# Moving the first sum of weights of 21 seven-product groups from VectorE to GpSimd

## The chip, the cores and the metric

The kernel runs as one program on one core of a Trainium2 chip. The metric is the device time of one execution in microseconds (us). The core has a matrix engine (TensorE, PE in the profile; its weight loads are listed as PEld), a vector engine (VectorE, DVE), a scalar engine (ScalarE, ACT), a general engine (GpSimd, POOL) and an engine that here does nothing but issue transfers (SyncE, SP). Each engine works through its own list of instructions in the order in which the program issued them, and waits on semaphores for the others.

## The reference

One layer of a diffusion backbone is computed for 128 context tokens and 128 latent tokens of width 2048: modulation, one wide input projection, two attention mixers, a merge, an output projection, and a feed-forward part with hidden width 8192. All of it is float32. What the change touches is the first half of the feed-forward part:

```python
def sq_relu_mlp(h, w_up, w_down):
    return jnp.square(jax.nn.relu(h @ w_up)) @ w_down

h2 = rms_norm(xp, norm2_w[l]) * (1 + sc2) + sh2
xp = xp + g2 * sq_relu_mlp(h2, w_up[l], w_down[l])
```

`h2` has 128 rows for each of the two token sets, `w_up` is 2048 x 8192 and `w_down` is 8192 x 2048.

## The kernel before

**Steps.** Weights are streamed. One step is one tile of 128 x 1024 float32 (512 KB): SP loads it into a buffer called `raw`, other engines prepare it, TensorE uses it. `add_step` puts a step on the list `wsteps` and `run` walks the list. For step i, `run` first issues the loads that are due (the digit string RUN says how many steps ahead), then the preparation of all steps up to i + LOOK[i] + 1 (LOOK is a digit string too, mostly 3 to 6 in the part that matters here), then the matmuls of step i, then whatever was hung on that step. This order of issue is the order on every engine; no scheduler changes it (`manual_schedule`).

**Precision.** A weight tile is split in two: ScalarE copies it to the type float32r (`wH`, the high part), and VectorE subtracts this from the tile (`wL`, the low part, line 230). Activations are split in the same way. Every product is then three matmuls: high by high, high by low, low by high. In 13 steps listed in LO_DMA the low part is made in another way: ScalarE writes minus the high part (line 236), and a transfer issued by GpSimd adds the weight to it in memory (`minus_plus`, line 237).

**Feed-forward.** The hidden width is taken in 8 pieces of 1024 columns, each as two blocks of 512. Piece p goes through an up stage, in which `h2 @ w_up` is made, and a down stage, in which it is multiplied into four column blocks of the output (`down_unit`). In the up stages of pieces 1 to 7 the eight positions of the inner dimension are of two kinds. At a plain position two weight tiles are used as they are (24 matmuls in two steps). At the positions listed in FAST a 2 x 2 block product is made with seven products in place of eight (21 matmuls in two steps). Such a group takes two tiles `X` and `Y`, and sums of weights have to be made first. There are 36 groups: 4, 5, 5, 5, 6, 5 and 6 in pieces 1 to 7.

**A group's preparation.** `prep_x` issues one ScalarE copy (`XH`). `prep_y` issues, in this order: on ScalarE half a copy of Y (`YB`, line 1045 by way of the helper at line 83); on VectorE the first sum `t13` = X + Y's left half repeated (line 1046, 128 x 1024); on ScalarE its high part `tH`; on VectorE three operations of 128 x 512 (lines 1049 to 1051), the first of which reads `t13`; on ScalarE the high part `uH`; on VectorE the three low parts `XL`, `tL`, `uL` (lines 1054 to 1056, 128 x 1024 each). `mm_x` and `mm_y` then use them: `XL` is read by the first matmuls of the group's x step, `tL` and `uL` in its y step. The tile `t13` is called `t` in the profile, X and Y are both called `raw`.

**GpSimd's list.** During the feed-forward part GpSimd has only transfers to issue: in 16 of the down units (SUM_DMA) a transfer that adds the unit's result to the running sum (line 1137), after ScalarE has copied that result out of the accumulators, and the transfers of line 237. All tiles of 128 x 1024, loaded, split and summed ones, come from one pool of 48 buffers of 4 KB per partition (`G`), so that an instruction that writes a tile also waits for whatever last used its buffer.

Of the kernel before, what the change touches and what calls it, by code (L numbers as in the profile page):

```python
# [34 lines left out]
FAST = {1: (0, 3, 5, 7), 2: (0, 2, 3, 6, 7), 3: (0, 2, 4, 5, 7), 4: (0, 2, 4, 5, 7), 5: (0, 1, 2, 3, 5, 7), 6: (0, 3, 4, 5, 7), 7: (0, 1, 2, 4, 6, 7)}  # L35
# [8 lines left out]
RUN = "210002222232246656665644343333334454433433345555544455434445554445665555555665443433234334444445665543321222222222444444444444442222222232333344444455544544444444443344343334455533344444444443255444444455556866544443566553333323333345552332222222223444332333333333332211122222332233322211233323323333333333333333332343322211333343333333333333444433543333322233333333322333233322222222322333443434455544333120222222222222344566655555455445322325335553333333"  # L44
CONST_AT = [59, 67]
XL_DMA = []
ADA_AT = [None, 4, 12, 21, 21, 32, 32, 37]
XS_AT = {1: 9, 2: 14, 3: 30}
POST = {('kvA', 0): [67, 68, 74], ('qA', 0): [70, 73, 75], ('qA', 1): [74, 76, 82], ('kB', 0): [76, 81, 87], ('qB', 0): [83, 84, 92], ('kB', 1): [84, 89, 92], ('qB', 1): [91, 94, 97]}
# [12 lines left out]
def tile_hybrid_step(ctx: ExitStack, tc: tile.TileContext, a):  # L62
# [8 lines left out]
    act, dve, pe, pool, sync = nc.scalar, nc.vector, nc.tensor, nc.gpsimd, nc.sync  # L71

    def G(name, dt=F32):
        return gp.tile([P, 1024], dt, name=name, tag="g")
# [7 lines left out]
    def copy(out, in_):  # L82
        act.activation(out, in_, AF.Copy)  # L83
# [311 lines left out]
    def mod_pair(f):  # L395

        box, k0 = {}, 2 * f
        if f == 0:
# [10 lines left out]
            return  # L409
        i = ADA_AT[f]  # L410
        for j in range(2):
# [569 lines left out]
    def up_pair(p):  # L981
# [32 lines left out]
        for pos, is_fast in enumerate(kinds):  # L1014
# [16 lines left out]
            def prep_x(b=b, pos=pos):  # L1031
                b["XH"] = G("XH", F32R)
                copy(b["XH"], b["x"]["raw"])
                if 8 * p + pos in XL_DMA:
                    b["XL"] = G("XL", F32R)
                    minus_plus(b["XL"], b["XH"], b["x"]["src"])

            def prep_y(b=b, pos=pos):
                X, Y = b["x"].pop("raw"), b["y"].pop("raw")
                b["YB"] = G("YB", F32R)  # L1040
                if "XL" not in b:
                    b["XL"] = G("XL", F32R)
                b["tH"], b["tL"], b["uH"], b["uL"] = (G(n, F32R) for n in ("tH", "tL", "uH", "uL"))
                t = G("t13")
                copy(b["YB"][:, 0:512], Y[:, 512:1024])
                dve.tensor_tensor(t.rearrange("p (a n) -> p a n", a=2), X.rearrange("p (a n) -> p a n", a=2),  # L1046
                                  Y[:, 0:512].unsqueeze(1).to_broadcast([P, 2, 512]), op=OP.add)
                copy(b["tH"], t)
                dve.tensor_tensor(Y[:, 0:512], t[:, 0:512], X[:, 512:1024], op=OP.add)
                dve.tensor_tensor(b["YB"][:, 512:1024], Y[:, 512:1024], b["YB"][:, 0:512].bitcast(F32), op=OP.subtract)  # L1050
                dve.tensor_tensor(Y[:, 512:1024], Y[:, 0:512], Y[:, 512:1024], op=OP.add)  # L1051
                copy(b["uH"], Y)
                if 8 * p + pos not in XL_DMA:
                    dve.tensor_tensor(b["XL"], X, b["XH"].bitcast(F32), op=OP.subtract)  # L1054
                dve.tensor_tensor(b["tL"], t, b["tH"].bitcast(F32), op=OP.subtract)
                dve.tensor_tensor(b["uL"], Y, b["uH"].bitcast(F32), op=OP.subtract)
# [45 lines left out]
            for i, (nm, pf, mf) in enumerate((("x", prep_x, mm_x), ("y", prep_y, mm_y))):  # L1102
                add_step(a["w_upF"][p - 1, j, i], mf, key)
                b[nm] = wsteps[-1]
                wsteps[-1]["prep"] = pf
# [253 lines left out]
```

## Time and profile before

| what | value |
|---|---|
| median of 3 runs | 1353.36 us (1353.11 to 1353.66) |
| the profiled execution, its own time | 1353.49 us |
| its span, first to last instruction | 1351.7 us |
| up stages of pieces 1 to 7, us from the start of the span | 703-745, 790-831, 876-916, 962-1002, 1046-1087, 1132-1172, 1218-1258 |
| VectorE's first sum (line 1046) | 36 times 1218 ns |
| ScalarE's high part of that sum (`tH`, line 83) | 36 times 1063 ns |
| GpSimd's compute instructions after 662 us | none |

The first group of a piece is prepared during the down stage ahead of it (piece 1's at 693.7 us). All durations come from one profiled execution, so sums are made against its own 1353.49 us. Times in the profile are microseconds from the first instruction. A matmul's listed duration (0.39 us) overlaps the next one's; the rate of TensorE is read from the distance of their starts. VectorE's neighbours overlap slightly in the same way: instructions listed with 1.22 us start 1.13 to 1.14 us apart when nothing holds them up. A note in brackets behind an instruction gives the idle time of its engine ahead of it, and what ended that.

### The profile page before, as it was taken

How to read it: one execution, taken by the hardware profiler on the slowest of the kernel's cores; microseconds unless marked ns; L12 is line 12 of the kernel's file. 1: busy time of each engine (PE TensorE's matmuls, PEld its weight loads, DVE VectorE, ACT ScalarE, POOL GpSimd, SP SyncE). 2: the span in 40 equal slices, each digit the busy share in tenths (PEclk: the TensorE clock that was granted, in tenths of full speed). 3: DMA queues.
4: the chain of work that ended last, by engine and by line, in shares of the span. 5: the costliest groups of instructions: out<-in, count | busy, mean ns of one | idle time of the engine just before them, and what ended most of it. 6: DMA issues, size and time to landing. Idle time of an engine off the chain costs nothing. (4 is left out here: it accounts for less than half of the span.)

```text
span 1351.7 us, 18516 instructions
## 1 busy us (share of the span) xinstructions
PE 1339.3 (99%) x6699; PEld 1086.3 (80%) x6701; DVE 1156.1 (86%) x1499; ACT 730.8 (54%) x955; POOL 60.0 (4%) x71
## 2 busy tenths in 40 slices
PE   8999999999999999999999999999999999999998
PEld 4777786888888878888888888888888888888887
DVE  4578787988798979997779998998999999899685
ACT  4534532476646535345657566566665656656640
POOL 0000000422000000000000000000000000000000
PEclk9999999999999999999999999999999999999999
DMA  9999979948568999998556666988786887769942
GB/s 379 408 409 408 401 278 321 353 147 306 179 263 318 345 407 372 354 328 277 202 203 218 249 224 229 294 272 289 234 285 218 264 286 210 279 190 312 343 151 94
DMA packets 108027, 381.78 MB, mean 282 GB/s; under 512 B 12192, under 2 KB 13152, under 8 KB 107936
## 3 DMA queue, kind: packets, MB, share of 16 engines
q1 hardware_dynamic: 103200, 364.00, 73.4%
q0 software_dynamic: 4592, 16.52, 6.4%
q8 instruction: 52, 0.85, 0.3%
q14 instruction: 39, 0.32, 0.1%
q10 hardware_dynamic: 144, 0.08, 0.0%
HBM read 365.06 MB, written 7.11 MB: 275 GB/s over the span
## 5 line engine op out<-in xcount | busy, mean ns | idle before, releaser
L230 DVE TENSOR_TENSOR wL<-raw,wH 128x1024 fp32r<-128x1024 f32 x370 | 440.4, 1221 | 106.9 <-ACT wH L83 98.3
L83 ACT ACTIVATE wH<-raw 128x1024 fp32r<-128x1024 f32 x384 | 387.3, 1053 | 165.4 <-PE acc L281 31.0
L375 PE MATMUL acc<-wH,hH 128*128 128x512 f32 x288 | 113.6, 394 | 0.6 <-ACT hH L83 0.6
L377 PE MATMUL acc<-wH,hL 128*128 128x512 f32 x288 | 112.3, 390 | 0.0
L376 PE MATMUL acc<-wL,hH 128*128 128x512 f32 x288 | 112.2, 389 | 0.0
L280 PE MATMUL acc<-wH,hH 128*128 128x512 f32 x256 | 101.3, 396 | 0.0
L282 PE MATMUL acc<-wH,hL 128*128 128x512 f32 x256 | 99.8, 390 | 0.0
L281 PE MATMUL acc<-wL,hH 128*128 128x512 f32 x256 | 99.7, 389 | 0.0
L83 ACT ACTIVATE tH<-t 128x1024 fp32r<-128x1024 f32 x36 | 38.3, 1063 | 67.5 <-DVE t L1046 62.7
L375 PEld LDWEIGHTS acc<-wH,hH 128*128 128x128 f32 x288 | 54.0, 188 | 15.1 <-issue 3.3
L377 PEld LDWEIGHTS acc<-wH,hL 128*128 128x128 f32 x288 | 54.1, 188 | 11.9 <-DVE hL L87 0.4
L376 PEld LDWEIGHTS acc<-wL,hH 128*128 128x128 f32 x288 | 54.1, 188 | 10.8
L1200 DVE CUSTOM_DVE_ANT_0 aT<-aT,cB,cols 128x1024 f32<-128x1024 f32 x48 | 61.1, 1281 | 0.2
L1200 DVE CUSTOM_DVE_ANT_0 junk<-aT,cB,cols 128x1024 bf16<-128x1024 f32 x48 | 61.2, 1284 | 0.0
L83 ACT ACTIVATE uH<-raw 128x1024 fp32r<-128x1024 f32 x36 | 38.3, 1063 | 35.3 <-DVE raw L1051 32.4
L282 PEld LDWEIGHTS acc<-wH,hL 128*128 128x128 f32 x256 | 48.0, 188 | 10.1
L281 PEld LDWEIGHTS acc<-wL,hH 128*128 128x128 f32 x256 | 48.1, 188 | 9.4
L280 PEld LDWEIGHTS acc<-wH,hH 128*128 128x128 f32 x256 | 48.1, 188 | 9.5
L297 PE MATMUL ps_ada<-araw,cpad 128*32 128x256 f32 x768 | 46.4, 382 | 3.6 <-DMA araw<-in_w_pair 3.0
L1046 DVE TENSOR_TENSOR t<-raw 128x1024 f32<-128x1024 f32 x36 | 43.9, 1218 | 3.2 <-DMA raw<-in_w_upF 1.8
L1099 ACT ACTIVATE up<-up 128x1024 f32<-128x1024 f32 x28 | 29.7, 1062 | 29.1 <-DVE up L1093 28.7
L1054 DVE TENSOR_TENSOR XL<-raw,XH 128x1024 fp32r<-128x1024 f32 x36 | 43.8, 1218 | 0.4 <-DMA dsum<-dsum 0.4
(621 smaller groups left out, 3244.1 us busy)
## 6 DMA issues: line engine op xcount, KB each, us to landing
raw<-in_w_in SPq DMA_DIRECT2D x136, 512.0 KB, 7.3
raw<-in_w_down SPq DMA_DIRECT2D x128, 512.0 KB, 5.8
araw<-in_w_pair SPq DMA_DIRECT2D x96, 512.0 KB, 10.2
raw<-in_w_upF SPq DMA_DIRECT2D x72, 512.0 KB, 5.0
aT<-in_w_gT SPq DMA_DIRECT2D x64, 512.0 KB, 7.1
raw<-in_w_up SPq DMA_DIRECT2D x56, 512.0 KB, 5.3
aT<-in_w_adaT SPq DMA_DIRECT2D x32, 512.0 KB, 6.9
raw<-in_w_out SPq DMA_DIRECT2D x32, 512.0 KB, 7.6
```

The lines of the kernel that those rows point to most:

```text
L83: act.activation(out, in_, AF.Copy)
L230: dve.tensor_tensor(st["lo"], st["raw"], st["hi"].bitcast(F32), op=OP.subtract)
L280: pe.matmul(acc[tb], sh, wh[:, k, :], start=f, stop=False)
L281: pe.matmul(acc[tb], sh, wl[:, k, :], start=False, stop=False)
L282: pe.matmul(acc[tb], sl, wh[:, k, :], start=False, stop=l)
L297: pe.matmul(box["ps"][32 * k:32 * k + 32, 256 * j:256 * j + 256], cpad[:, 4 * q + k, :], raw[:, k, :], start=j == 0 and q == 0, stop=j == ...
L375: pe.matmul(acc[tb], sh, wh[:, k, :], start=kt == 0 and k == 0, stop=False)
L376: pe.matmul(acc[tb], sh, wl[:, k, :], start=False, stop=False)
L377: pe.matmul(acc[tb], sl, wh[:, k, :], start=False, stop=last and k == 1)
L1046: dve.tensor_tensor(t.rearrange("p (a n) -> p a n", a=2), X.rearrange("p (a n) -> p a n", a=2), Y[:, 0:512].unsqueeze(1).to_broadcast([P, ...
L1054: dve.tensor_tensor(b["XL"], X, b["XH"].bitcast(F32), op=OP.subtract)
L1200: dve.tensor_tensor_reduce(out, box["raw"], cB[s, h, tag], 1.0, dst if h else baT[:, part, fb:fb + 1], OP.mult, OP.add, dst)
```

## The change

In the groups of the odd pieces 1, 3, 5 and 7 (4, 5, 6 and 6 groups, 21 in all) the first sum is issued to GpSimd in place of VectorE. The instruction, its operands and its place in the order of issue stay as they are; nothing else is moved. In pieces 2, 4 and 6 (15 groups) it stays on VectorE.

```diff
+T_POOL = [8 * p + pos for p in (1, 3, 5, 7) for pos in FAST[p]]
...
                 t = G("t13")
                 copy(b["YB"][:, 0:512], Y[:, 512:1024])
-                dve.tensor_tensor(t.rearrange("p (a n) -> p a n", a=2), X.rearrange("p (a n) -> p a n", a=2),
+                (pool if 8 * p + pos in T_POOL else dve).tensor_tensor(t.rearrange("p (a n) -> p a n", a=2), X.rearrange("p (a n) -> p a n", a=2),
                                   Y[:, 0:512].unsqueeze(1).to_broadcast([P, 2, 512]), op=OP.add)
                 copy(b["tH"], t)
```

## The prediction

> **What bounds the kernel now.** First the page's line of busy times, then a table of the four up stages in which the change lies (pieces 1, 3, 5, 7).
>
> ```profile
> span 1351.7 us, 18516 instructions
> PE 1339.3 (99%) x6699; PEld 1086.3 (80%) x6701; DVE 1156.1 (86%) x1499; ACT 730.8 (54%) x955; POOL 60.0 (4%) x71
> ```
> ```profile
> 703.00:745.00 42.00, 42.00 (x190) 34.80 (x189) 37.43 (x42) 28.19 (x33) 0.94 (x1) 1.00 0.63 206
> 876.00:916.00 40.00, 40.00 (x178) 33.15 (x177) 37.27 (x40) 23.68 (x27) 1.72 (x2) 1.00 0.83 274
> 1046.00:1087.00 41.00, 41.00 (x191) 34.20 (x190) 38.94 (x43) 25.48 (x31) 1.72 (x2) 1.00 0.86 277
> 1218.00:1258.00 40.00, 39.48 (x175) 32.37 (x174) 39.44 (x42) 23.87 (x28) 0.86 (x1) 1.00 0.88 310
> sum 163.00, PE 162.48 PEld 134.52 DVE 153.08 ACT 101.22 POOL 5.23; mean PE 40.62 PEld 33.63 DVE 38.27 ACT 25.30 POOL 1.31
> ```
>
> Columns are stretch, length, then busy time of PE, PEld, DVE, ACT and POOL. TensorE is idle for 0.52 us of the 163.00 (163.00 - 162.48), at the full granted clock (1.00). Busy could hide slow issue, so I looked at the distance of starts too: the p = 3 rows further down show two `tL` matmuls, three apart, at 903.14 and 903.82, so 0.227 us each. At that rate the stage is bound by TensorE's own work, and nothing that a faster VectorE delivers can be used. But VectorE is close behind: 153.08 us of 163.00.
>
> So the question is one-sided: what can the change take from TensorE, not what can it give.
>
> **The change part by part.** *What VectorE is rid of.* Piece 1's second group:
>
> ```profile
> 713.45 1.22 DVE L1046 TENSOR_TENSOR t<-raw 128x1024 f32<-128x1024 f32 x1
> 714.70 0.69 DVE L1049 TENSOR_TENSOR raw<-t,raw 128x512 f32<-128x512 f32 x1
> ```
>
> The next operation reads `t` and so starts 1.25 us after it. If nothing else happened, VectorE would win 1.25 us per group, 26 us in 21 groups.
>
> *What GpSimd's sum costs VectorE.* No such sum runs on GpSimd before, but GpSimd did run work that reads memory beside VectorE: the masks of the bias at 241 us. The first fence is GpSimd's timeline, the second VectorE's.
>
> ```profile
> 247.23 0.55 POOL L522 TENSOR_SCALAR_AFFINE_SELECT bias<-bias 64x384 f32<-64x384 f32 x1
> 247.74 1.53 POOL L520 TENSOR_SCALAR_AFFINE_SELECT bias<-bias 64x384 f32<-64x384 f32 x1
> 249.33 1.42 POOL L522 TENSOR_SCALAR_AFFINE_SELECT bias<-bias 64x384 f32<-64x384 f32 x1
> ```
> ```profile
> 246.68 0.68 DVE L541 TENSOR_REDUCE ssq<-sq 128x4 f32<-128x512 f32 x1
> 247.28 3.05 DVE L230 TENSOR_TENSOR wL<-raw,wH 128x1024 fp32r<-128x1024 f32 x2
> ...
> 720.04 2.35 DVE L230 TENSOR_TENSOR wL<-raw,wH 128x1024 fp32r<-128x1024 f32 x2
> ```
>
> Beside the reduction, which reads one tile, a mask took 0.55 us and the reduction was on time (0.68). Beside the subtractions, which read two tiles in memory, each mask took 1.42 to 1.53, and the pair of subtractions took 3.05 us against 2.35 for the same pair elsewhere: 0.35 us more for each of the two masks. The two engines exclude each other: the mask that comes at 247.74 stands until the subtraction begun at 247.28 is through, then runs, and the next subtraction stands meanwhile. All seven VectorE operations of a group read two streams from memory (`raw`, `t`, `XH` and so on), so this holds for every one of them.
>
> How long will a sum hold VectorE off? A mask reads 384 elements per partition and costs VectorE 0.35 us, 0.91 ns each. The sum reads two streams of 1024. If both come at once, 1024 x 0.91 = 0.93 us (lower end). If they come one after the other, 2048 x 0.91 = 1.87 us. By the mask's own undisturbed 0.55 us less a fixed 0.10 (the shortest fill below), 0.45/384 = 1.17 ns, 2.40 us; with the fixed part in, 0.55/384 = 1.43 ns, 2.93 us (upper end).
>
> ```profile
> L118 POOL MEMSET inv<- 128x1 f32 x1 | 0.1, 98 | 0.0
> ```
>
> I take 2.1, between 1.87 and 2.40, as the mask is the nearest row and I see no reason why two inputs should be read at once by an engine whose one input already shuts VectorE out. [...]
>
> So VectorE loses 2.1 - 1.25 = 0.85 us per group where it was to win.
>
> *Where that reaches TensorE.* VectorE falls behind by 0.85 us with each group, less what its own idle gaps swallow. Those in the odd pieces:
>
> ```profile
> 706.16 1.22 DVE L230 TENSOR_TENSOR wL<-raw,wH 128x1024 fp32r<-128x1024 f32 x1 [3.48 <-ACT wH L83]
> 887.38 1.23 DVE L230 TENSOR_TENSOR wL<-raw,wH 128x1024 fp32r<-128x1024 f32 x1 [1.90 <-DMA dsum<-dsum]
> 1040.39 1.22 DVE L1046 TENSOR_TENSOR t<-raw 128x1024 f32<-128x1024 f32 x1 [0.75 <-PE acc L282]
> 1047.58 1.29 DVE L724 TENSOR_TENSOR a8L<-ps_T,a8H 128x512 fp32r<-128x512 f32 x2 [0.51 <-ACT a8H L83]
> 1053.63 1.23 DVE L1054 TENSOR_TENSOR XL<-raw,XH 128x1024 fp32r<-128x1024 f32 x1 [0.38 <-DMA dsum<-dsum]
> 1229.53 1.23 DVE L1046 TENSOR_TENSOR t<-raw 128x1024 f32<-128x1024 f32 x1 [0.18 <-PE Q L993]
> ```
>
> And the tightest place of each piece: the low part as VectorE makes it, and the first matmul that reads it (pieces 1, 3, 5, 7 in this order).
>
> ```profile
> 736.64 1.22 DVE L1056 TENSOR_TENSOR uL<-raw,uH 128x1024 fp32r<-128x1024 f32 x1
> 741.15 0.39 PE L992 MATMUL Q<-uL,sH 128*128 128x512 f32 x1
> ```
> ```profile
> 898.31 1.22 DVE L1054 TENSOR_TENSOR XL<-raw,XH 128x1024 fp32r<-128x1024 f32 x1
> 899.44 1.22 DVE L1055 TENSOR_TENSOR tL<-t,tH 128x1024 fp32r<-128x1024 f32 x1
> 901.10 0.39 PE L992 MATMUL Q<-XL,h21H 128*128 128x512 f32 x1
> 903.14 0.39 PE L992 MATMUL Q<-tL,sH 128*128 128x512 f32 x1
> 903.82 0.39 PE L992 MATMUL Q<-tL,sH 128*128 128x512 f32 x1
> ```
> ```profile
> 1060.24 1.22 DVE L1054 TENSOR_TENSOR XL<-raw,XH 128x1024 fp32r<-128x1024 f32 x1
> 1061.37 1.22 DVE L1055 TENSOR_TENSOR tL<-t,tH 128x1024 fp32r<-128x1024 f32 x1
> 1061.90 0.39 PE L992 MATMUL Q<-XL,h21H 128*128 128x512 f32 x1
> 1063.94 0.39 PE L992 MATMUL Q<-tL,sH 128*128 128x512 f32 x1
> ```
> ```profile
> 1250.46 1.22 DVE L1056 TENSOR_TENSOR uL<-raw,uH 128x1024 fp32r<-128x1024 f32 x1
> 1254.07 0.39 PE L992 MATMUL Q<-uL,sH 128*128 128x512 f32 x1
> ```
>
> The margin is the matmul's start less the end of the low part. One more thing shifts the lag: GpSimd does not wait for VectorE's turn. It takes the next group's sum as soon as X, Y and the buffer are there, and may so put 2.1 us ahead of `tL` and `uL` of the group before, ahead of the saving that goes with it. I give each piece without and with such an early sum.
>
> Piece 1: the gap of 3.48 swallows the first group; three groups make 2.55, the margin is 741.15 - 737.86 = 3.29. Loss 0.
>
> Piece 3: two groups (1.7) go into the gap of 1.90. Then two more (1.7), and a delay of 1.03 in GpSimd's queue:
>
> ```profile
> 895.29 0.86 POOL L237 DMA_DIRECT2D wL<-in_w_up  x1 [17.45 <-DVE uL L1056]
> 895.12 1.22 DVE L1046 TENSOR_TENSOR t<-raw 128x1024 f32<-128x1024 f32 x1
> ```
>
> The transfer of line 237 is ahead of the fourth sum in the order of issue, so GpSimd is free for it at 896.15, where VectorE began at 895.12. Behind the late sum stand `tH` on ScalarE and lines 1049 to 1056 on VectorE. Lag 2.73, margin of `XL` 901.10 - 899.53 = 1.57: loss 1.2. With the fifth sum ahead of `tL`: 4.83 against 903.14 - 900.66 = 2.48, loss 2.35. I take 1.8. GpSimd's own transfers can in turn stand behind a sum: the one whose landing ends the gap at 887.38 would then land later, and that gap would swallow less, up to the 1.7 that I put into it; this stays in the range.
>
> Piece 5: four groups (3.4) less the gaps 0.75, 0.51 and 0.38 (1.64) leave 1.76, against 1061.90 - 1061.46 = 0.44: loss 1.3. With an early fifth sum 3.86 against 1063.94 - 1062.59 = 1.35: loss 2.5. I take 1.9.
>
> Piece 7: six groups (5.1) less 0.18, 4.92, against 1254.07 - 1251.68 = 2.39 at its last group, which no sum follows: loss 2.5.
>
> Sum 0 + 1.8 + 1.9 + 2.5 = 6.2 us (5.0 to 7.35 at a hold of 2.1). The down stages and the even pieces, which have no such sum, let VectorE catch up before the next odd piece, and I price them at nothing; if they don't, piece 3's first two groups would start with what is left.
>
> The profiled execution took 1353.49 us (span 1351.7), 0.13 above the median of 1353.36. **Forecast 1353.49 + 6.2 = 1359.7 us**, 0.5% slower.
>
> With the hold at 1.87 the same four sums give 2.2 to 4.2, at 2.40 (0.3 us more per group) 9 to 12. The forecast's own range is 1355.6 to 1365.5.
>
> **The rivals.** *Not slower.* GpSimd reads both streams at once, and holds VectorE off for 0.93 us. Then VectorE gains 0.32 per group (1.25 - 0.93), its lag never grows, and TensorE goes on at 0.227 us a matmul. The most there is to win is TensorE's 0.52 us of idleness: 1353.0 to 1353.5. It decides from a hold of 1.25 us downwards; up to some 1.7 us the margins still swallow most. For it: two inputs at once are what VectorE itself does (1.22 us for two streams of 1024). Against it: one input alone already shut VectorE out.
>
> *Much slower.* The hold is the upper 2.93, so 1.68 lost per group. Piece 1 then loses 5.04 - 3.29 = 1.7, piece 3 carries 1.46 over its gap and loses 1.46 + 3.36 + 1.03 - 1.57 = 4.3, piece 5 6.72 - 1.64 - 0.44 = 4.6, piece 7 10.08 - 0.18 - 2.39 = 7.5: 18 us, 1371.6; with early sums some 4 more. For it: GpSimd's fixed part may belong to the hold. Against it: VectorE lost 0.35, not 0.55, to a mask.
>
> *The sum does not move*: no; all 21 numbers are positions in FAST, and nothing in the group depends on the engine.
>
> *Faster by more than 0.2%* (2.7 us) would need idleness of TensorE that the stages don't have (0.52).
>
> **How the numbers follow.** 0.2% is about what a measurement of this kernel can tell from no change. The forecast's case has 0.73, not slower 0.13, much slower 0.11, faster 0.03. The lower edge of the forecast's own range, 2.2 us, lies just within 0.2%, which adds 0.03: same 0.16, slower 0.81, faster 0.03. For 8 times in 10 the range takes in the edge of no change and leaves out most of the heavy case: 1353.2 to 1369.0.
>
> **What would show it.** Right: 21 sums on POOL of 2.2 us or more; VectorE operations of 3.1 to 3.4 us in place of 1.22 beside them; TensorE's idle time near 1 to 3 us in each of pieces 3, 5 and 7 and none in piece 1; `tH` on ScalarE waiting for POOL. Wrong: VectorE's operations at 1.22 us beside GpSimd's sums, or TensorE late by more than 1 us in piece 1, or a loss in the down stages.

## The result, and the profile after

| kernel | median | runs | profiled execution | span |
|---|---|---|---|---|
| before, same chip | 1353.23 us | 4 | 1353.49 us (shown ahead) | 1351.7 us |
| changed | 1376.40 us (1373.82 to 1378.08) | 4 | 1375.87 us | 1374.1 us |

The change makes the kernel slower by a factor of 1.017 (95% interval 1.0154 to 1.0185), that is by 23 us. The forecast was 6.2 us, and 1376.4 lies above the range's end of 1369.0.

In the changed kernel all lines from the sum on stand one lower in the file: the sum is L1047, the three half-width operations L1050 to L1052, the low parts L1055 to L1057. First the page, then the table of stretches (columns as before), with the four up stages at their new places and two short stretches in piece 3.

```profile
span 1374.1 us, 18564 instructions
...
PE 1347.6 (98%) x6699; PEld 1089.0 (79%) x6701; DVE 1157.2 (84%) x1478; ACT 728.3 (53%) x955; POOL 115.5 (8%) x92
...
L1047 POOL TENSOR_TENSOR t<-raw 128x1024 f32<-128x1024 f32 x21 | 57.6, 2741 | 105.8 <-DMA raw<-in_w_upF 32.1
```
```profile
703.00:745.00 42.00, 42.00 (x191) 34.84 (x190) 34.12 (x36) 28.06 (x33) 8.69 (x4) 1.00 0.60 207
878.00:925.00 47.00, 42.99 (x179) 34.99 (x178) 40.42 (x37) 23.28 (x27) 12.08 (x6) 0.93 0.75 234
1055.00:1100.00 45.00, 39.16 (x164) 30.86 (x163) 35.48 (x35) 23.30 (x29) 12.43 (x6) 0.92 0.75 225
1230.00:1276.00 46.00, 43.39 (x189) 34.76 (x188) 41.51 (x40) 24.67 (x30) 14.40 (x6) 1.00 0.86 283
...
907.00:913.00 6.00, 6.00 (x16) 4.66 (x17) 5.97 (x7) 3.94 (x5) 0.00 (x0) 0.54 0.37 112
913.00:919.00 6.00, 6.00 (x28) 4.99 (x27) 4.71 (x5) 2.20 (x3) 0.00 (x0) 1.00 0.93 319
```

The 21 sums are there, 2.74 us each on the mean. TensorE now stands for several us in pieces 3, 5 and 7 (4.0, 5.8 and 2.6 us of these stretches). And something shows that no step of the prediction had: the granted clock (last but two) is 0.93 in piece 3 and 0.92 in piece 5. It is 0.54 in the 6 us that follow the longest stand, with 16 matmuls where the next 6 us have 28.

Who waited for whom? First VectorE's waits, then TensorE's (total, times, longest).

```profile
DVE raw L1050 <- POOL t L1047: 22.9, 7, 4.3
```
```profile
PE Q L993 <- DVE XL L1055: 9.5, 4, 4.0
...
PE acc L281 <- DVE up L1094: 1.3, 2, 1.0
```

VectorE, which the prediction expected to be held off beside GpSimd's sums (2.1 us each), also stood idle seven times until GpSimd's sum was there. Of the 22.9 us, 18.35 are five waits for a sum that GpSimd began right after issuing a transfer (VectorE started again at 735.26 after 4.07, 901.52 after 3.44, 1052.17 after 3.29, 1082.36 after 4.27, 1242.69 after 3.28). The other two, in piece 7, were for sums whose weights had just been loaded.

The longest stand of TensorE, in piece 3, can be read link by link. GpSimd's timeline (with two sums of piece 1 ahead of it for comparison, and behind it one of piece 5 to which the last section comes back), then VectorE's, ScalarE's and TensorE's:

```profile
703.92 2.41 POOL L1047 TENSOR_TENSOR t<-raw 128x1024 f32<-128x1024 f32 x1 [14.93 <-DVE wL L231]
717.32 2.91 POOL L1047 TENSOR_TENSOR t<-raw 128x1024 f32<-128x1024 f32 x1 [10.99 <-PE Q L993]
...
898.17 0.88 POOL L238 DMA_DIRECT2D wL<-in_w_up  x1 [7.65 <-DVE uL L1057]
898.78 2.70 POOL L1047 TENSOR_TENSOR t<-raw 128x1024 f32<-128x1024 f32 x1
902.42 2.59 POOL L1047 TENSOR_TENSOR t<-raw 128x1024 f32<-128x1024 f32 x1 [0.94 <-PE Q L993]
...
1057.22 2.71 POOL L1047 TENSOR_TENSOR t<-raw 128x1024 f32<-128x1024 f32 x1
```
```profile
716.74 1.22 DVE L1056 TENSOR_TENSOR tL<-t,tH 128x1024 fp32r<-128x1024 f32 x1
717.87 3.44 DVE L1057 TENSOR_TENSOR uL<-raw,uH 128x1024 fp32r<-128x1024 f32 x1
...
735.26 0.69 DVE L1050 TENSOR_TENSOR raw<-t,raw 128x512 f32<-128x512 f32 x1 [4.07 <-POOL t L1047]
...
901.52 0.69 DVE L1050 TENSOR_TENSOR raw<-t,raw 128x512 f32<-128x512 f32 x1 [3.44 <-POOL t L1047]
...
902.84 2.71 DVE L1052 TENSOR_TENSOR raw<-raw 128x512 f32<-128x512 f32 x1
905.48 1.21 DVE L1055 TENSOR_TENSOR XL<-raw,XH 128x1024 fp32r<-128x1024 f32 x1
```
```profile
894.76 1.06 ACT L84 ACTIVATE uH<-raw 128x1024 fp32r<-128x1024 f32 x1 [3.15 <-DVE raw L1052]
895.73 1.04 ACT L84 ACTIVATE wH<-raw 128x1024 fp32r<-128x1024 f32 x1
896.81 1.06 ACT L237 ACTIVATE wL<-wH 128x1024 fp32r<-128x1024 f32 x1
```
```profile
902.35 0.39 PE L992 MATMUL Q<-XH,h21H 128*128 128x512 f32 x1
906.75 0.80 PE L993 MATMUL Q<-XL,h21H 128*128 128x512 f32 x1 [4.01 <-DVE XL L1055]
907.34 0.63 PE L994 MATMUL Q<-XH,h21L 128*128 128x512 f32 x1
907.77 0.63 PE L992 MATMUL Q<-XH,sH 128*128 128x512 f32 x1
...
912.46 0.42 PE L994 MATMUL Q<-tH,sL 128*128 128x512 f32 x1
912.72 0.39 PE L992 MATMUL Q<-uH,h21H 128*128 128x512 f32 x1
```

1. ScalarE's `uH` waits 3.15 us for VectorE's L1052 of the group before. Behind `uH`, in order, stand `wH` and the minus copy (L237), done at 897.87.
2. GpSimd's transfer needs that copy and goes at 898.17. The fourth group's sum stands behind it in GpSimd's list and starts at 898.78. VectorE waits for it until 901.52.
3. The fifth group's sum starts at 902.42. It catches VectorE in L1052, which takes 2.71 us in place of 0.69, so `XL` is done only at 906.69.
4. TensorE, ready since its matmul of 902.35, goes on at 906.75. The distance of starts is 4.40 us where 0.227 is usual: a stand of 4.17 us.
5. From 907.34 to 912.46 twelve distances (907.34 to 907.77 is the first) make 5.12 us, 0.427 each; at 912.46 to 912.72 the old pace is coming back. Twelve times 0.200 us is 2.4 us; another 0.36 go between 906.75 and 907.34 (0.59 in place of 0.227). Together 2.8 us.

In piece 5 the same chain runs from a transfer at 1079.02 to a TensorE stand from 1083.71 to 1087.73, again with slow matmuls behind it.

### The profile page after: what moved, and what is told of

The parts are those of the page before. It is cut to its first block, busy times and chain, and to the rows that moved or that the text cites. A ratio compares the mean times of both kernels' runs of the same rounds, so it can differ in the third digit from the quotient of the medians.

```text
span 1374.1 us, 18564 instructions
## 1 busy us (share of the span) xinstructions
PE 1347.6 (98%) x6699; PEld 1089.0 (79%) x6701; DVE 1157.2 (84%) x1478; ACT 728.3 (53%) x955; POOL 115.5 (8%) x92
## 4 chain that ended last, share of the span: by engine, by line
PE 84%; DMA 5%; DVE 5%; issue 4%; POOL 1%; ACT 1%; SPq 0%; POOLq 0%; DVEq 0%; ACTq 0%
PE acc L281 15%; PE acc L282 15%; PE acc L283 15%; PE Q L993 5%; PE Q L994 4%; PE Q L992 4%; PE acc L376 4%; PE acc L378 4%; PE acc L377 4%; PE ps_ada L298 3%; DMA araw<-in_w_pair 2%; DVE wL L231 1%; POOL t L1047 1%; PE ps_T L722 1%; DMA dsum<-dsum 1%
## 5 line engine op out<-in xcount | busy, mean ns | idle before, releaser
L231 DVE TENSOR_TENSOR wL<-raw,wH 128x1024 fp32r<-128x1024 f32 x370 | 449.7, 1248 | 108.8 <-ACT wH L84 102.8
L84 ACT ACTIVATE tH<-t 128x1024 fp32r<-128x1024 f32 x36 | 38.1, 1060 | 69.7 <-POOL t L1047 30.5
L1047 POOL TENSOR_TENSOR t<-raw 128x1024 f32<-128x1024 f32 x21 | 57.6, 2741 | 105.8 <-DMA raw<-in_w_upF 32.1
L1055 DVE TENSOR_TENSOR XL<-raw,XH 128x1024 fp32r<-128x1024 f32 x36 | 48.3, 1340 | 2.1 <-DMA dsum<-dsum 2.1
L1057 DVE TENSOR_TENSOR uL<-raw,uH 128x1024 fp32r<-128x1024 f32 x36 | 48.3, 1341 | 0.0
```

Of the source, the lines that this page charges most:

```text
L231: dve.tensor_tensor(st["lo"], st["raw"], st["hi"].bitcast(F32), op=OP.subtract)
L1047: (pool if 8 * p + pos in T_POOL else dve).tensor_tensor(t.rearrange("p (a n) -> p a n", a=2), X.rearrange("p (a n) -> p a n", a=2), Y[:, ...
```

## The experiments

Three explanations competed for the 17 us that the forecast lacked: sums that are late because of a transfer ahead of them in GpSimd's list; the hold alone (VectorE's operations stretched beside GpSimd's sums, as `uL` to 3.44 us beside the sum of 717.32), larger or more often than thought; and the slow matmuls behind a long stand. A position is written 8p + pos: 29 is position 5 of piece 3. All times are set against runs of the kernel before on the same chip. Line numbers move a little from kernel to kernel, so rows are best followed by the names of their tiles.

**Clear sums only.** The 14 sums that are not in the next experiment.

```diff
-T_POOL = [8 * p + pos for p in (1, 3, 5, 7) for pos in FAST[p]]
+T_POOL = [8, 11, 13, 24, 28, 31, 40, 43, 47, 56, 57, 60, 62, 63]
```

> GpSimd makes only the 14 sums that have no accumulating transfer right ahead of them in its list; the other seven go back to VectorE. Theory Q (the losses add up in one chain: a sum that stands behind a transfer comes late, VectorE waits for it, and the next sum then holds VectorE off again, so that a margin which each would leave intact is used up): the waits of 3.3 to 4.3 us of VectorE for a sum behind a transfer vanish, no TensorE stall over 2 us is left, and the loss falls from 22 us to 2 to 6 us: 1355 to 1359. Rival H (each sum costs its hold of VectorE, 2.2 us against 1.25 saved, and the loss goes with their number): 14/21 of 22 us, about 15 us: 1368.

Measured 1357.13 us against 1352.72, ratio 1.0031 [1.002, 1.0043]: +4.4 us. VectorE waited for a sum three times, 6.0 us in all, and TensorE's largest distance of starts was 1.8 us.

**The others only.** The seven sums that have an accumulating transfer right ahead of them inside the piece. (The first sum of piece 3 follows a transfer too, at 866.51; VectorE had other work then and didn't wait, so it is among the fourteen.)

```diff
+T_POOL = [15, 26, 29, 41, 42, 45, 58]
```

> The complement: GpSimd makes only the seven sums that stand right behind a transfer in its list. Theory Q: VectorE still waits some 2 to 4 us for each of them, but with the neighbours on VectorE the margins of 1.6 to 3.3 us swallow most: 1 to 5 us, 1354 to 1358, and this loss and that of the other 14 together are well under 22 us. A form of Q in which the transfers alone do the damage: 12 us or more, 1365. Rival H: 7/21 of 22 us, 7 us: 1360, and the two losses add up to 22.

Measured 1357.18 us against 1352.72, ratio 1.0027 [1.0017, 1.0038]: +4.5 us. The waits are all there, as VectorE's view of waits for this kernel shows:

```profile
DVE raw L1050 <- POOL t L1047: 20.6, 6, 4.1
```

Nearly the same 20.6 us of waiting as in the full change (22.9), and a fifth of the loss. So late sums alone do not explain the 23 us. Together the two parts lose 8.9 us when each runs alone, and 23 when both are in. What is missing appears only when both are in; whether it comes where one group's late sum and the next group's sum fall on the same stretch is tried further down.

**All 21, but each sum ahead of the transfers.** Where a sum on GpSimd is among the next steps to be prepared, an accumulating transfer is kept back and issued right behind that sum, or at the latest after three (line 238 of the changed kernel) or six steps (line 1138).

```diff
-        pool.dma_start(lo, src.bitcast(F32R), accum_op=OP.add)
+        pool_dma(lambda: pool.dma_start(lo, src.bitcast(F32R), accum_op=OP.add))
...
-                pool.dma_start(dsum[n], part, accum_op=OP.add)
+                pool_dma(lambda: pool.dma_start(dsum[n], part, accum_op=OP.add), 6)
```

> All 21 sums on GpSimd, but its transfers are issued behind the next sum where one follows within a few steps (all three transfers of line 237 that stood ahead of a sum, and the four of line 1137 where a sum follows). Theory Q: the waits of 3.3 to 4.3 us behind a transfer go (15 us of the 22.9 us that VectorE waits for GpSimd's sums), the stalls of 4 us of TensorE go and with them the slow clock behind them; loss 5 to 11 us, 1358 to 1364. Rival H: the holds are as many as before: 18 to 22 us, 1371 to 1375.

Measured 1359.27 us against 1352.72, ratio 1.0045 [1.003, 1.006]: +6.5 us. VectorE's waits for a sum fell to 11.6 us, the largest distance of TensorE's starts is 1.41 us, and no matmul was slow. The order of GpSimd's list carries about 16.5 of the 23 us; with the transfers out of the way the loss is of the size that was forecast for the hold.

**Two sums off: the late ones of the chain.** Positions 29 and 45 go back to VectorE, the sums begun at 898.78 and 1079.63.

```diff
+T_POOL = [8 * p + pos for p in (1, 3, 5, 7) for pos in FAST[p] if 8 * p + pos not in (29, 45)]
```

> As the changed kernel, but the two sums that stand behind a transfer of line 237 in the middle of pieces 3 and 5 are VectorE's again (19 on GpSimd). Theory Q with C (a late sum plus the next sum's hold make the two stalls of 4 us, and each of these brings some 2.5 us of slow matmuls): both stalls fall under 2 us and no slow matmul is left: 22 us less 2 x (4 + 2.5) = 9 us and up to 3 more for what the neighbours then lose: 1362 to 1365. Rival H (by number, 19/21): 20 us, 1373.

Measured 1362.26 us against 1352.8, ratio 1.0072 [1.0057, 1.0087]: +9.5 us. Two of the 21 sums carry 13.7 us (23.2 less 9.5). No matmul is slow, and the largest distance is 1.8 us.

**Two sums off: the ones behind them.** Positions 31 and 47, the sums begun at 902.42 and 1083.96. The late sums stay.

```diff
+T_POOL = [8 * p + pos for p in (1, 3, 5, 7) for pos in FAST[p] if 8 * p + pos not in (31, 47)]
```

> As the changed kernel, but the two sums that follow the late ones, those of the last groups of pieces 3 and 5, are VectorE's again (19 on GpSimd); the late sums stay on GpSimd. Theory Q with C: the late sums are waited for as before (some 3.4 and 4.3 us), but no hold comes on top, so that each stall falls by about 2 us, to some 2 us, with or without slow matmuls behind it: 22 us less 2 x 2.2, and up to 2 x 2.5 less again: 13 to 18 us, 1366 to 1371. Rival L (the late sum alone makes the stall): 22 us, 1375. Rival H: 20 us, 1373.

Measured 1366.44 us against 1352.8, ratio 1.0094 [1.0077, 1.0111]: +13.6 us by the medians, 12.7 by the ratio (its four runs spread from 1363.84 to 1368.93, and the trace is of the longest). So the second link, the hold of L1052 ahead of `XL` in piece 3 (2.71 us in place of 0.69) and of `XL` itself in piece 5 (3.38 in place of 1.22), is worth some 10 us of the 23, though VectorE's waits are as long as ever (23.2 us in seven). TensorE's two stands shrank to distances of 2.36 and 1.86 us. The first was still followed by eight slow matmuls. TensorE's timeline at that place, and the table of stretches of the same kernel:

```profile
906.19 0.50 PE L993 MATMUL Q<-XL,h21H 128*128 128x512 f32 x1 [1.97 <-DVE XL L1055]
```
```profile
906.00:910.00 4.00, 3.81 (x10) 3.00 (x11) 4.00 (x5) 2.56 (x4) 0.00 (x0) 0.57 0.81 264
```

**Stands without GpSimd.** To measure the slow matmuls by themselves, the kernel before was given repeats of `XL` on VectorE, three to seven more of the same subtraction, in one group each of five pieces (position 44 is no group, so its entry does nothing).

```diff
+MORE = {18: 3, 29: 4, 36: 5, 44: 4, 51: 6, 60: 7}
...
-                    dve.tensor_tensor(b["XL"], X, b["XH"].bitcast(F32), op=OP.subtract)
+                    for _ in range(1 + MORE.get(8 * p + pos, 0)):
+                        dve.tensor_tensor(b["XL"], X, b["XH"].bitcast(F32), op=OP.subtract)
```

> The kernel before, all sums on VectorE, with the subtraction that makes XL repeated in one group of each of the pieces 2 to 7 (3, 4, 5, 4, 6 and 7 times more, the same result), so that TensorE waits once in each piece, for 1 to 6 us. Theory C (a TensorE stall of about 4 us or more is followed by some 12 matmuls at 0.43 us in place of 0.227, which costs 2.4 us more; a shorter one is not): slow matmuls behind the stalls of 4 us and over, none behind those under 3 us. Rival D (the slow matmuls of the changed kernel came from GpSimd's work or from a chance throttle): none behind any stall, or behind all of them.

One run, 1377.65 us against 1352.72. TensorE's timeline in piece 2 and in piece 4, and the stretches behind the stands of pieces 3 and 4:

```profile
806.84 0.39 PE L992 MATMUL Q<-XH,h21H 128*128 128x512 f32 x1
808.77 0.50 PE L993 MATMUL Q<-XL,h21H 128*128 128x512 f32 x1 [1.54 <-DVE XL L1056]
809.11 0.40 PE L994 MATMUL Q<-XH,h21L 128*128 128x512 f32 x1
809.34 0.39 PE L992 MATMUL Q<-XH,sH 128*128 128x512 f32 x1
...
991.04 0.39 PE L992 MATMUL Q<-XH,h21H 128*128 128x512 f32 x1
993.39 0.67 PE L993 MATMUL Q<-XL,h21H 128*128 128x512 f32 x1 [1.96 <-DVE XL L1056]
993.85 0.63 PE L994 MATMUL Q<-XH,h21L 128*128 128x512 f32 x1
994.28 0.63 PE L992 MATMUL Q<-XH,sH 128*128 128x512 f32 x1
```
```profile
908.00:912.00 4.00, 4.00 (x11) 3.14 (x12) 4.00 (x4) 0.00 (x0) 0.00 (x0) 0.57 0.22 76
994.00:998.00 4.00, 4.00 (x13) 3.18 (x12) 3.97 (x5) 1.06 (x1) 0.00 (x0) 0.63 0.40 119
```

GpSimd does nothing in these stretches (0.00 us busy), and slow matmuls came all the same, behind a standing TensorE. After a distance of 1.93 us (piece 2) the next starts are 0.23 apart, after 2.35 us (piece 4) they are 0.43 apart. The stand of about 4 us that was expected to be needed was too long: a distance of 2.35 us was enough here, and 1.93 us was not.

**The stands filled.** All 21 sums, and ten matmuls with a zero tile, which add nothing to Q, ahead of the first matmul of each group whose `XL` is late.

```diff
+FILL = {29: 10, 45: 10}
...
+                for _ in range(FILL.get(8 * p + pos, 0)):
+                    pe.matmul(box["Q1"], zero[:, 0:P], zero, start=False, stop=False)
```

> As the changed kernel, all 21 sums on GpSimd, but TensorE has ten matmuls with zeros (10 x 0.227 = 2.3 us) right ahead of each of the two places where it stands for 4 us; they add nothing to the result. Theory C (standing brings the slow clock): the places of standing fall to under 2 us and no slow matmul follows; the filling itself costs nothing, as TensorE would have stood: 22 us less 2 x 2.4, about 17 us: 1370 to 1371. Rival D (the slow matmuls come with GpSimd's work, or by chance): slow matmuls stay and the loss is 22 us or more, 1375.

Measured 1370.51 us against 1352.8, ratio 1.0131 [1.0115, 1.0146]: +17.7 us, 5.5 less than with the change alone. TensorE's timeline and the stretch of piece 3:

```profile
903.08 2.11 PE L1066 MATMUL Q<-zero 128*128 128x512 bf16 x9
904.83 0.58 PE L995 MATMUL Q<-XH,h21H 128*128 128x512 f32 x1
907.23 0.50 PE L996 MATMUL Q<-XL,h21H 128*128 128x512 f32 x1 [1.81 <-DVE XL L1058]
907.56 0.40 PE L997 MATMUL Q<-XH,h21L 128*128 128x512 f32 x1
907.80 0.39 PE L995 MATMUL Q<-XH,sH 128*128 128x512 f32 x1
```
```profile
880.00:925.00 45.00, 43.12 (x190) 34.55 (x190) 40.91 (x39) 23.53 (x27) 11.06 (x5) 1.00 0.77 242
```

`XL` comes no earlier (907.23 against 906.75), yet the matmuls behind it are 0.24 us apart and the granted clock is 1.00 in the whole stage. TensorE still stood, for distances of 2.40 us here and 2.05 us in piece 5. This is the price of the slow matmuls by itself: 5.5 us measured, 2.7 and 2.9 us less lost in pieces 3 and 5 than with the change alone, and twice 2.8 us in the trace of the change.

**Half sums.** GpSimd makes the left half of the sum, VectorE the right.

```diff
+                if 8 * p + pos in T_POOL:
+                    pool.tensor_tensor(t[:, 0:512], X[:, 0:512], Y[:, 0:512], op=OP.add)
+                    dve.tensor_tensor(t[:, 512:1024], X[:, 512:1024], Y[:, 0:512], op=OP.add)
```

> GpSimd makes the left half (512 columns) of each of the 21 sums, VectorE the right half. Hold theory: GpSimd holds VectorE off for the time in which it reads, 2.2 us for 2 x 1024 elements, so 1.0 to 1.2 us for half, seen as VectorE operations of 2.2 to 2.4 us in place of 1.22, and its sums take some 1.3 to 1.5 us. VectorE then loses 1.1 and saves 0.5 to 0.6 a group. Theory Q (losses add up beyond the margins, so that the loss falls faster than the hold): 2 to 7 us, 1355 to 1360, no slow matmuls. Rival H (in proportion): half of 22 us, 1364. Rival F (GpSimd's cost is mostly fixed): hold near 2 us, loss 20 us and more.

Measured 1357.35 us against 1353.25, ratio 1.0036 [1.0022, 1.005]: +4.1 us. VectorE's timeline in piece 1:

```profile
716.64 2.32 DVE L1060 TENSOR_TENSOR tL<-t,tH 128x1024 fp32r<-128x1024 f32 x1
718.89 1.21 DVE L1061 TENSOR_TENSOR uL<-raw,uH 128x1024 fp32r<-128x1024 f32 x1
```

`tL` is held for 1.10 us (2.32 less 1.22), half of the 2.22 that a whole sum cost (3.44 less 1.22). With half of the elements read, two streams of 512, the hold was half: about 1.08 ns for each element in both. VectorE saves 0.47 us on a half (its next operation starts 0.78 us after the start of its half sum at 722.29, against 1.25 us after a whole one) and pays 1.1, so halving cannot turn the loss into a gain.

No variant came under the kernel before, and none could win much: TensorE's 0.52 us of idle time in the four stages is all that there was to have.

## Why the prediction was wrong

**What bounds the kernel, and the sign: right.** Nothing that VectorE was rid of showed in the time, and every kernel with a sum on GpSimd was slower.

**The hold: right.** Taken 2.1 us, measured 2.2. In piece 1 the sum of 717.32 stretched `uL` to 3.44 us, 0.04 above the 3.1 to 3.4 that were named as a sign. The rival with 0.93 us (both streams read at once) is out, and so is the one with 2.93: its 1371.6 us is the nearest of the three times to 1376.4, but by a hold that isn't there. The masks' loss scaled by elements read (1.87 us) and their undisturbed time without its fixed part (2.40) did bracket it. One reading behind them was thin: the mask of 247.23, taken as one beside the reduction, overlaps it for 0.13 us only and runs on beside the first subtraction. The hold comes close to the length of a whole sum: 2.2 us, beside the 2.41 us of the sum of 703.92, during which VectorE stood idle. And `uL` ends 1.08 us behind the sum that held it (721.31 and 720.23), nearly the 1.13 us that lie between two starts of its kind.

**The delay in GpSimd's queue, priced in one place only: the step that failed.** The prediction counted one sum behind a transfer in all the pieces, and 1.03 us for it (transfer at 895.29, GpSimd free at 896.15, VectorE's own sum at 895.12). At all other places it put the delay at nothing, without a reason. But the trace before has the same order there. Pieces 1 and 5, GpSimd's timeline and then VectorE's:

```profile
731.92 0.94 POOL L237 DMA_DIRECT2D wL<-in_w_down  x1 [70.45 <-ACT wL L236]
...
1066.66 0.86 POOL L237 DMA_DIRECT2D wL<-in_w_up  x1 [18.83 <-PE Q L993]
```
```profile
731.18 1.22 DVE L1046 TENSOR_TENSOR t<-raw 128x1024 f32<-128x1024 f32 x1
...
1065.91 1.22 DVE L1046 TENSOR_TENSOR t<-raw 128x1024 f32<-128x1024 f32 x1
```

Counted in the same way these are delays of 1.68 and 1.61 us, and in piece 7 a transfer at 1220.43 beside the sum at 1220.41 makes 0.88. With its 1.68 piece 1 would have had a lag of 4.23 us in place of 2.55, more than its margin of 3.29. In the changed kernel VectorE waited at five places, 3.3 to 4.3 us each: first for the delay (0.55 to 1.54 us from its last operation to the start of the sum), then for the whole 2.7 us of the sum. Less the 1.25 us saved, that is 2.0 to 3.0 us a place, where four of the five had been priced at 0.85. In piece 3 itself the price was nearly right, 0.85 + 1.03 = 1.88 against 3.44 - 1.25 = 2.19: the transfer went 2.88 us later than before (898.17), as it waits for ScalarE's minus copy, behind `uH`, which waits for VectorE's L1052; but VectorE came 2.96 us later too, so the delay did not grow.

With the transfers put behind the sums the loss fell from 23 to 6.5 us, so this step is where the forecast missed. Piece 1 then lost nothing, nor did it with the clear sums only; with the seven others it lost 1.6 us. That the forecast of 6.2 fits the kernel with the transfers behind is partly luck: VectorE still waits 11.6 us there, and pieces 1, 3, 5 and 7 lose 0, 2.5, 1.4 and 0.9 us (by the starts of the same matmuls in the trace before) where 0, 1.8, 1.9 and 2.5 were forecast.

**The early fifth sum: right in kind, put one place too late.** It was set ahead of `tL`, where the margin is 2.48 us, with a loss of 2.35. It came two operations ahead of that, at L1052 and so ahead of `XL`, whose margin is 1.57. Taking it off in pieces 3 and 5 won back about 10 us. In piece 5 the place that the prediction watched lost what it said: TensorE's distances of 1.13 and 1.80 us, the second ending at 1073.60, are 2.5 us beyond the usual, against 1.3 to 2.5. The stand of 4.02 us came one group later, behind the transfer at 1079.02 that had not been counted.

**Margins: priced alone, they are shared.** The fourteen clear sums lose 4.4 us alone, the seven others 4.5, and all of them 23. Pieces 3 and 5 each hold both links of the chain. That this is why the losses do not simply add is argued from the traces; the runs with 29 and 45 or with 31 and 47 taken off show it for these two places.

**The clock: a term that was missing.** The slow matmuls behind the two long stands cost 5.5 us of the 23, and no step of the prediction has them.

**By pieces.** Distances of TensorE's starts beyond their usual 0.227 us, added up by piece in the trace of the change:

| piece | predicted | measured | of which slow matmuls |
|---|---|---|---|
| 1 | 0 | 1.3 | 0 |
| 3 | 1.8 | 6.9 | 2.8 |
| 5 | 1.9 | 9.8 | 2.8 |
| 7 | 2.5 | about 3 | 0 |

They make 21, against 22.4 us that the span has grown (1374.1 less 1351.7); the rest was not traced to a place. Piece 7, where the hold alone was priced, came out within half a us, but VectorE also waited 3.28 us there for a sum behind a transfer, so that is partly luck. Piece 1 was to lose nothing, and a loss of more than 1 us there was named as a sign of error; it lost 1.3, behind the sum that VectorE awaited for 4.07 us until 735.26. TensorE's wait there is the one for L1094 in the list above: VectorE clears the accumulators late, and the down stage stands for 1 us at its start. A loss in the down stages had been named as a sign of error as well. The other sign given, `tH` on ScalarE waiting for POOL, came true (12 times, 30.5 us).

## What to carry to other kernels

Before moving an operation to an idle engine, walk that engine's own list in order: what stands ahead of the new instruction, whom does that wait for, and does that wait hang on the very work that the move delays? Do so at every place and not at one: the places that were passed over here stood in the trace before in the same way. Where the old engine has nothing else to do, it waits for the delay and for the new engine's whole operation (3.3 to 4.3 us at five places here), not for a hold of 2.2 us alone. And two small losses on one chain must be priced together, since each alone can fit into a margin that both need. In these traces TensorE's stands of 1.96 us and more by the listed idle time also had slow matmuls behind them, 0.43 us apart in place of 0.227.

## What the hardware showed unexpectedly

**TensorE was slow behind short stands.** These are the stands by the idle time that the profile lists. Followed by matmuls 0.43 us apart: 4.01 and 3.63 us in the change, 3.28 and 1.96 with the repeated `XL`, 1.97 with positions 31 and 47 off. Not followed: 1.41 and 1.31 in the change, 1.54, 1.53 and 1.53 with the repeats, and 1.81 in the kernel with the stands filled. So of these stands all of 1.96 us and more were followed by slow matmuls, and none of 1.81 us and less. By the distances of starts the two kinds overlap, as 2.40 us in the filled kernel did no harm and 2.35 did elsewhere; but the matmul ahead of the 2.40 is listed with 0.58 us in place of 0.39. The slow part lasted for 7 to 12 matmuls (the four stretches shown above around such a part have a granted clock of 0.54 to 0.63), and then the matmuls were 0.23 us apart again.

**Beside operations that read the accumulators the hold did not show.** At 1057.22 GpSimd made a sum of 2.71 us, and VectorE's operations beside it, which read `ps_T` in the accumulators, took their usual time:

```profile
1057.52 1.28 DVE L725 TENSOR_TENSOR a8L<-ps_T,a8H 128x512 fp32r<-128x512 f32 x2
```

Two in 1.28 us, as in the trace before (1.29). It was the same at 1231.53, with a sum of 2.41 us beside a pair listed with 1.28 us. In these two places operations with one input in the accumulators were not held.
